# Modulation columns by transposes and a VectorE sum, and a new set of ordering numbers, in a two-layer attention backbone

## The chip, the cores and the metric

One core of a Trainium2 chip runs the whole program. The metric is the device time of one execution in microseconds (us). TensorE does matmuls and transposes, VectorE (DVE in the profile) and ScalarE (ACT) read PSUM and work on SBUF, GpSimd (POOL) works on SBUF alone, and SyncE (SP) issues most of the loads from HBM.

## The reference

Two layers work on 512 latent tokens `x` and 256 context tokens, 1024 wide. Layer 0 is differential attention with 8 heads (two softmaxes of head width 64, the second taken off with weight lambda, then a norm of each head's output). Layer 1 is grouped-query attention with 8 query heads and 2 key/value heads of width 128, norms of queries and keys, and latent outputs alone. All is in fp32.

```python
m = silu(cvec) @ ada_w[i] + ada_b[i]          # shift, scale, gate: 3 x 1024, for c and for c_ctx
h = rms_norm(x, pre_g[i]) * (1 + scale) + shift
q, k, v, z = split(h @ w_in)                  # rope on latent q and k
o = softmax(q k^T / sqrt(d)) v                # latent queries read latent and context keys
x = x + gate * rms_norm((o * silu(z)) @ w_out[i], post_g[i])
```

## The kernel before, in words

Activations are kept with features on the partitions (`h` tiles of 128 features x 768 tokens). Each large product is done as three fp32r matmuls (`mm3`, L147 to L149): both operands are split into a rounded part (`hi`) and a rest (`lo`), and hi x hi, hi x lo and lo x hi are summed in PSUM. A weight is loaded into a `raw` tile by SP, ScalarE casts it to `hi` (L210), and VectorE or GpSimd subtracts to get `lo` (L204). PSUM has eight banks: four single ones, `bk0` to `bk3`, handed out in turn (`trp` for a short use, `pj` until `close`), and two pairs `sc0`, `sc1` for scores (`sc2`). In the program's listing they are `bk_68` to `bk_71` and `sc_72`, `sc_73`.

**Start.** `x_norm` (L548) squares x on ScalarE, adds on VectorE, sums over partitions by an fp32 matmul with ones, and gets `rsb` by Ln and Exp. The modulation of layer 0 comes from `cols4`: silu(c) and silu(c_ctx) are the two columns of a 32-wide stationary tile, and four such tiles run side by side on 32 columns of the array each, so the product lies on rows 0, 1, 32, 33, 64, 65, 96, 97 of a bank. `ada_red` (L490) copies it to `row` and turns it into columns: for each block of 128 features one fp32 matmul with `row` stationary and `sel32` (128 x 2) moving adds the four partial rows and transposes at once (L497). `mods_set` adds bias and norm gain. `ht` (L574) makes an `h` tile: `hf` on VectorE (L579), `hi` on ScalarE (L580), `lo` on VectorE (L581). `w_split` (L527) splits the first weights, and `lam_setup` (L611) loads the rope table and lambda.

**Layer 0.** For each head there are score units (L845, L874: one block of 128 queries, two softmaxes; VectorE takes the maximum at L850, ScalarE the exponential at L853), then transposes of the probabilities (L910, copied to `ah` by ScalarE at L913 and to `al` by VectorE at L914), then PV matmuls (L154). L931 and L942 belong to the norm of a head's output. Projections of later heads are filled in between, and so is the modulation of layer 1 and the gate of layer 0 (`grp_mm`, L701; `ada1_finish`, L714; `gate0_finish`, L979, which broadcasts a row over the partitions with an fp32 matmul by `selb`).

**Between the layers** the output projection runs, `h1_tr` transposes the normed tokens (L1196), and a hand-written list `KV` orders key tiles `k`, value tiles `v`, transposes of the last tokens `t` and of keys `c`. A key tile holds its bank until `k_rope` has read it (`kn`, L1276), which waits for two squares on ScalarE (L1254) and two operations on GpSimd (L1256, L1257).

**Layer 1** has score units (scores L147 to L149 with `kh`, `qh`; maximum L1384, scaling of the maximum L1387, exponential L1390 into `p`), query transposes `q_tr` (L1341, cast `qh` at L1344), transposes of `p` (L1405) and PV. VectorE sums the gate of layer 1 (`gate1_part`, L1445), and `gate1_finish` splits it (cast L376 on ScalarE, subtraction L377 on GpSimd) and sums it over partitions.

**What sets the order.** A planner, `flow`, keeps its own clock in us. Each step has a due time (from `ATT`, `TS`, `AT1`, `GAP0`, `DL0`, and lags `LA`, `LT`, `LM`, `SLAG`, `SLAG1`, `QLAG`, `ACD` behind other steps); while nothing is due it takes a piece of the next projection in `FILL0` (from `HF0`) or `FILL1`. `GFIN` says after which score units `gate1_finish` may come. After that the tile framework schedules each engine's queue, led by priorities: `HOT`, `HOT0`, `HOT1`, `WARM` and `PRI` say how far a step is moved ahead. `AGB` is the number of buffers for the first modulation weights.

Of the kernel before, what the change touches and what calls it, by code (L numbers as in the profile page):

```python
# [28 lines left out]
HOT = 500
HF0 = ((('qk', 1), ('qk', 2), ('z', 0)), (('qk', 3),), (('z', 1), ('v', 2), ('qk', 4), ('z', 2)), (('qk', 5), ('z', 3)), (('v', 4), ('qk', 6), ('z', 4)), (('qk', 7), ('z', 5)), (('v', 6), ('z', 6)), (('z', 7),))  # L30
# [1 line left out]
ATT = 15.0
ACCN = (0, 0, 3, 3, 3, 3, 3, 3)
ACD = 5.0
FILL1 = (('z', 0), ('q', 2), ('q', 1), ('z', 2), ('z', 1), ('q', 3), ('z', 3), ('z', 4), ('z', 5), ('z', 7), ('z', 6))
HOT0 = (4200, 3100, 0, 4800)
HOT1 = (1100, 2900, 2600, 2600, 2100)
WARM = 5400
AGB = 11
PRE = 14.0  # L40
TS = 9.0
# [2 lines left out]
KV = (('k', 0), ('k', 1), ('k', 2), ('t', 0), ('k', 3), ('t', 1), ('v', 0), ('v', 1), ('c', 0), ('v', 2), ('c', 1), ('k', 4), ('c', 2), ('k', 5), ('c', 3), ('v', 3), ('v', 4), ('c', 4), ('v', 5), ('c', 5))
SPL = 8.0
GAP0 = 8.0
DL0 = (0.0, 0.0, 0.0, 0.0, 0.0, 0.0, -1.5, 3.0)
# [35 lines left out]
def tile_backbone(  # L83
# [406 lines left out]
    def ada_red(k0, nb, o):  # L490
        n = 2 * nb
        row = st.tile([P, 512], F32, tag="row", name=nm("row"), bufs=1)[:, :n * P]
        nc.scalar.copy(row, o)
        close(o)
        o = trp()
        for b in range(n):
            nc.tensor.matmul(o[:, b * 2:b * 2 + 2], row[:, b * P:(b + 1) * P], sel32, start=b == 0, stop=b == n - 1)  # L497
# [29 lines left out]
    def w_split(q, r):  # L527
        parts = [(wq, q * 256, 0, 256), (wk0, q * 256, 256, 256), (wv0[q // 2], q % 2 * 512, 512, 512)]
        for (hi, lo), c, a, n in parts:
            nc.scalar.copy(hi[:, c:c + n], r[:, a:a + n])  # L530
# [18 lines left out]
    rsb = st.tile([P, T], F32, name="rsb")  # L549

    def x_norm(v):
        n = (S, C)[v]
        per = 1024 // n
        a, b = ((0, S), (S, T))[v]
        o = trp()[:, :n]
        for c in range(KT // per):
# [5 lines left out]
            nc.tensor.matmul(o, ones, sq[:, :n], start=c == 0, stop=c == KT // per - 1)
# [1 line left out]
        nc.scalar.activation(rsb[:, a:b], rsb[:, a:b], AF.Exp, scale=-0.5)

# [116 lines left out]
    with tc.tile_pool(name="t0", bufs=1) as t0:  # L682
# [27 lines left out]
        def ada1_finish(layer, sec):  # L710
            r = rows.pop((layer, sec))
            o = trp()
            for b in range(4):
                nc.tensor.matmul(o[:, 2 * b:2 * b + 2], r[:, b * P:(b + 1) * P], sel32, start=b == 0, stop=b == 3)  # L714
            ov_ = o[:, :8].rearrange("p (k v) -> p v k", v=2)
# [256 lines left out]
        def gate0_finish(half):  # L972
            r = rows.pop((0, 4 + half))
            sl = slice(half * 512, half * 512 + 512)
            b = bcast(ada_b[0, 2 * D + half * 512:2 * D + half * 512 + 512])
            g = bcast(post_g[0, sl])
            for v in range(2):
                o = trp()
                nc.tensor.matmul(o, selb[v], r, start=True, stop=True)  # L979
# [674 lines left out]
```

## Time and profile before

| | us |
|---|---|
| median of 3 runs | 826.17 |
| lowest and highest | 823.46, 826.22 |
| the profiled execution | 825.35 |
| its span, first to last instruction | 823.6 |
| TensorE busy | 794.6 |
| VectorE, ScalarE, GpSimd busy | 522.8, 451.5, 319.0 |

A row of a group reads: line, engine, operation, output<-inputs, shapes, count, then busy time in us (the union of the spans), mean ns of one, and the idle time before them with what ended it. A row of the time line reads: start, duration, engine, line, operation, and in brackets the idle time before it. Matmuls overlap, so the mean of one is longer than what it adds to the busy time.

### The profile page before, as it was taken

To read this page: it belongs to the slowest core of one execution; us is meant where nothing else is said; L and a number is where in the kernel's file an instruction comes from. 1 tells how busy PE (TensorE), PEld (TensorE's weight loads), DVE (VectorE), ACT (ScalarE), POOL (GpSimd) and SP (SyncE) were. 2 spreads that over 40 slices of the span, in tenths; PEclk is the share of its full clock that TensorE was granted. 3 is DMA by queue.
4 is the path that set the end of the run, shared out by engine and by line. 5 is a ranking of instruction groups with operands and counts; after the bars stand their busy time and mean duration, and the time that the engine had idled before them with its cause. 6 is when DMAs were issued, how large, how long until landed. Compare 5 with 4: busy or idle time off the path is not lost. (4 is left out here: it accounts for less than half of the span.)

```text
span 823.6 us, 14197 instructions
## 1 busy us (share of the span) xinstructions
PE 794.6 (96%) x5436; PEld 698.8 (85%) x5436; DVE 522.8 (63%) x941; ACT 451.5 (55%) x985; POOL 319.0 (39%) x436
## 2 busy tenths in 40 slices
PE   7999999999999999999999999999999999999997
PEld 4787878798877898887988898889989899888986
DVE  3756667865869535777367952566787756665534
ACT  5524358574575643665456753564355755676631
POOL 1112544742446522363712401574446434343101
PEclk9999999999999999999999999999999999999999
DMA  9924201222143322413320042041641310111112
GB/s 344 356 75 155 88 14 53 79 76 77 35 133 128 116 78 65 142 50 133 108 94 26 27 176 81 2 135 48 198 140 51 103 52 2 61 43 52 46 32 102
DMA packets 35235, 77.75 MB, mean 94 GB/s; under 512 B 3424, under 2 KB 10336, under 8 KB 35168
## 3 DMA queue, kind: packets, MB, share of 16 engines
q1 hardware_dynamic: 31600, 71.71, 25.9%
q10 hardware_dynamic: 3568, 5.16, 1.7%
q8 instruction: 42, 0.69, 0.3%
q14 instruction: 25, 0.20, 0.1%
HBM read 70.56 MB, written 2.10 MB: 88 GB/s over the span
## 5 line engine op out<-in xcount | busy, mean ns | idle before, releaser
L147 PE MATMUL bk<-whi,h 128*128 128x256 f32 (+1 forms) x592 | 176.7, 301 | 2.0 <-DVE kn L1276 1.8
L148 PE MATMUL bk<-wlo,h 128*128 128x256 f32 (+1 forms) x592 | 175.7, 299 | 0.3 <-DVE wlo L204 0.3
L149 PE MATMUL bk<-whi,h 128*128 128x256 f32 (+1 forms) x592 | 174.1, 298 | 0.1
L147 PE MATMUL bk<-h,whi 128*128 128x512 f32 (+2 forms) x416 | 147.8, 356 | 3.9 <-ACT sq L942 1.5
L149 PE MATMUL bk<-h,wlo 128*128 128x512 f32 (+2 forms) x416 | 144.6, 348 | 0.3 <-DVE wlo L204 0.3
L148 PE MATMUL bk<-h,whi 128*128 128x512 f32 (+2 forms) x416 | 144.8, 348 | 0.0
L218 POOL TENSOR_SCALAR p<-p,sm 128x768 f32<-128x768 f32 (+1 forms) x80 | 67.9, 851 | 147.4 <-DVE sm L856 48.6
L147 PEld LDWEIGHTS bk<-whi,h 128*128 128x128 f32 x592 | 112.1, 190 | 10.8 <-issue 3.6
L148 PEld LDWEIGHTS bk<-wlo,h 128*128 128x128 f32 x592 | 112.2, 190 | 4.3 <-DVE wlo L204 0.5
L149 PEld LDWEIGHTS bk<-whi,h 128*128 128x128 f32 x592 | 111.4, 189 | 3.9 <-DVE h L1209 0.3
L204 DVE TENSOR_TENSOR wlo<-raw,whi 128x1024 fp32r<-128x1024 f32 (+2 forms) x65 | 81.3, 1250 | 42.8 <-ACT whi L210 39.2
L147 PEld LDWEIGHTS bk<-h,whi 128*128 128x128 f32 x416 | 78.1, 188 | 18.8 <-issue 4.8
L210 ACT CAST whi<-raw 128x1024 fp32r<-128x1024 f32 x64 | 67.3, 1052 | 41.6 <-PE bk L148 14.7
L149 PEld LDWEIGHTS bk<-h,wlo 128*128 128x128 f32 x416 | 78.2, 188 | 8.4 <-issue 0.8
L148 PEld LDWEIGHTS bk<-h,whi 128*128 128x128 f32 x416 | 78.3, 188 | 6.7 <-issue 0.5
L853 ACT ACTIVATE p<-sc,sm 128x768 f32<-128x768 f32 (+1 forms) x68 | 59.6, 879 | 42.3 <-DVE sm L850 42.0
L850 DVE TENSOR_REDUCE sm<-sc 128x1 f32<-128x768 f32 (+1 forms) x68 | 60.7, 917 | 17.9 <-PE sc L845 17.9
L204 POOL TENSOR_TENSOR qr<-qr,rope 128x256 f32<-128x256 f32 x28 | 27.8, 1014 | 78.7 <-DMA sw<-qr 78.0
L204 POOL TENSOR_TENSOR sz<-sz,za 128x192 f32<-128x192 f32 (+1 forms) x48 | 31.8, 683 | 62.1 <-ACT za L184 61.5
L1409 DVE TENSOR_TENSOR al<-bk,ah 128x512 fp32r<-128x512 f32 x48 | 32.1, 685 | 23.9 <-ACT ah L1408 23.0
L845 PE MATMUL sc<-qk,qk 64*128 64x384 f32 (+1 forms) x396 | 46.5, 356 | 0.2 <-POOL qk L204 0.2
L861 DVE SCALAR_TENSOR_TENSOR p<-p,sm,p 128x768 f32<-128x768 f32 (+1 forms) x34 | 39.0, 1148 | 10.7 <-POOL p L218 8.9
(236 smaller groups left out, 1678.1 us busy)
## 6 DMA issues: line engine op xcount, KB each, us to landing
raw<-in_a_w SPq DMA_DIRECT2D x28, 512.0 KB, 3.5
araw<-in_ada_w SPq DMA_DIRECT2D x12, 1024.0 KB, 5.2
raw<-in_b_w SPq DMA_DIRECT2D x20, 512.0 KB, 4.0
ag<-in_ada SPq DMA_DIRECT2D x16, 512.0 KB, 7.5
raw<-in_w_out SPq DMA_DIRECT2D x16, 512.0 KB, 3.5
sw<-qr ACTq DMA_DIRECT2D x32, 128.0 KB, 2.1
gw<-in_ada_w SPq DMA_DIRECT2D x8, 512.0 KB, 4.5
xnt<-in_xlT SPq DMA_DIRECT2D x4, 512.0 KB, 5.5
```

Of the source, the lines that this page charges most:

```text
L147: nc.tensor.matmul(o, ahi, bhi, start=start, stop=False)
L148: nc.tensor.matmul(o, ahi, blo, start=False, stop=False)
L149: nc.tensor.matmul(o, alo, bhi, start=False, stop=stop)
L204: eng.tensor_tensor(dst[:, i:i + n], a[:, i:i + n], b[:, i:i + n], op)
L210: nc.scalar.copy(hi, r)
L218: (nc.vector if eng == "v" else nc.gpsimd).tensor_scalar(dst, src, s_, 1.0, ALU.mult, ALU.mult)
L845: prev = nc.tensor.matmul(sc[m][:, j if nk == T else m, :w], a[r, tok], b[r, c], start=i == 0, stop=i == 2)
L850: nc.vector.tensor_reduce(mx, scv, AX.XY if nk == T else AX.X, ALU.max, negate=True)
L853: nc.scalar.activation(pv_, scv, AF.Exp, bias=mx, accum_out=l[:, m:m + 1])
L861: nc.vector.scalar_tensor_tensor(ps_[0], pt, r, ps_[0], ALU.mult, ALU.add)
L1409: nc.vector.tensor_tensor(al, tr, f32(ah), ALU.subtract)
```

## The change

Five edits of the code, and new values for most of the ordering numbers.

1. `row_cols` takes the place of the `sel32` matmuls in `ada_red` and `ada1_finish`: each block of 128 features is transposed whole (a 128 x 128 transpose with `ident` moving), and VectorE adds rows 0, 32, 64, 96 and rows 1, 33, 65, 97 by one reduction into a small tile, which `mods_set` and `mod_cols` then read in place of PSUM.
2. `gate0_finish` splits the row into `rh` and `rl` and does two fp32r matmuls for each one in fp32; `selb` becomes fp32r.
3. `x_norm` of the context adds its two halves on VectorE and does one matmul in place of two.
4. The casts of `w_split` are ordered after the Exp of `x_norm(0)`.
5. `lam_setup` (subg, rope table, lambda) is called one pair later in the source.

```diff
-ACD = 5.0
+ACD = 1.89
-AGB = 11
+AGB = 10
-KV = (('k', 0), ('k', 1), ('k', 2), ('t', 0), ('k', 3), ('t', 1), ('v', 0), ('v', 1), ('c', 0), ('v', 2), ('c', 1), ('k', 4), ('c', 2), ('k', 5), ('c', 3), ('v', 3), ('v', 4), ('c', 4), ('v', 5), ('c', 5))
+KV = (('k', 0), ('k', 1), ('k', 2), ('t', 0), ('v', 0), ('k', 3), ('c', 0), ('t', 1), ('v', 1), ('v', 2), ('c', 1), ('k', 4), ('c', 2), ('k', 5), ('v', 3), ('v', 4), ('c', 3), ('c', 4), ('v', 5), ('c', 5))
-SLAG = (4.5, 1.5)
-SLAG1 = 2.9
+SLAG = (4.5, -0.05)
+SLAG1 = 4.96
-GFIN = (6, 12)
+GFIN = (10, 15)
...
-        o = trp()
+        mods_set(k0, nb, row_cols(row, n).rearrange("p (w k v) -> p w v k", w=2, k=nb))
+
+    def row_cols(r, n):
+        o = trp()[:, :n * P]
         for b in range(n):
-            nc.tensor.matmul(o[:, b * 2:b * 2 + 2], row[:, b * P:(b + 1) * P], sel32, start=b == 0, stop=b == n - 1)
-        ov_ = o[:, :2 * n].rearrange("p (w k v) -> p w v k", w=2, k=nb)
-        mods_set(k0, nb, ov_)
+            nc.tensor.transpose(o[:, b * P:(b + 1) * P], r[:, b * P:(b + 1) * P], ident)
+        cols_ = small(2 * n)
+        nc.vector.tensor_reduce(
+            cols_.rearrange("p (b r) -> p b r", b=n), o.rearrange("p (b j r) -> p b r j", j=4, r=32)[:, :, 0:2, :], AX.X, ALU.add)
+        return cols_
...
-            nc.scalar.copy(hi[:, c:c + n], r[:, a:a + n])
+            with after(last[0]):
+                nc.scalar.copy(hi[:, c:c + n], r[:, a:a + n])
...
-            if v:
+            if v == 0:
+                nc.tensor.matmul(o, ones, sq[:, :n], start=c == 0, stop=c == KT // per - 1)
+            elif c:
+                nc.vector.tensor_tensor(sq[:, :512], sq[:, :512], sq0[:, :512], ALU.add)
                 nc.vector.tensor_tensor(sq[:, :n], sq[:, :n], sq[:, n:512], ALU.add)
-            nc.tensor.matmul(o, ones, sq[:, :n], start=c == 0, stop=c == KT // per - 1)
+                nc.tensor.matmul(o, ones, sq[:, :n], start=True, stop=True)
+            sq0 = sq
...
-            if pr == 1:
+            if pr == 2:
                 lam_setup()
...
+            rh, rl = (t0.tile([P, 512], F32R, tag="tmp", name=nm("rg"), bufs=3) for _ in range(2))
+            nc.scalar.copy(rh, r)
+            nc.vector.tensor_tensor(rl, r, f32(rh), ALU.subtract)
             for v in range(2):
                 o = trp()
-                nc.tensor.matmul(o, selb[v], r, start=True, stop=True)
+                nc.tensor.matmul(o, selb[v], rh, start=True, stop=False)
+                nc.tensor.matmul(o, selb[v], rl, start=False, stop=True)
```

In the built programs the instructions move as the next three places show. Line numbers of the new program are its own (up to 13 higher).

VectorE before the first `h` tile, before the change: `wlo` are the rests of the first weights, `mods` the modulation columns.

```order
L559 TENSOR_TENSOR sqx_187<-sqx_187 128x512
L204 TENSOR_TENSOR wlo_137<-raw_152,whi_136 128x256
L204 TENSOR_TENSOR wlo_139<-raw_152,whi_138 128x256
L507 SCALAR_TENSOR_TENSOR mods<-bk_71,abT 128x2
L508 TENSOR_TENSOR mods<-bk_71,abT 128x2
L509 TENSOR_TENSOR mods<-mods,pre 128x2
L579 SCALAR_TENSOR_TENSOR hf_224<-xnt,mods,rsb 128x512
L204 TENSOR_TENSOR wlo_141<-raw_152,whi_140 128x512
```

The same place after the change:

```order
L567 TENSOR_TENSOR sqx_187<-sqx_187 128x512
L502 TENSOR_REDUCE sm_211<-bk_71 128x4
L512 SCALAR_TENSOR_TENSOR mods<-sm_211,abT 128x2
L513 TENSOR_TENSOR mods<-sm_211,abT 128x2
L204 TENSOR_TENSOR wlo_137<-raw_152,whi_136 128x256
L514 TENSOR_TENSOR mods<-mods,pre 128x2
L204 TENSOR_TENSOR wlo_139<-raw_152,whi_138 128x256
L591 SCALAR_TENSOR_TENSOR hf_226<-xnt,mods,rsb 128x512
```

The reduction is new, the modulation columns come ahead of the weight rests, and the second weight rest still stands ahead of `hf`.

ScalarE at the first score units of layer 1, before the change: `ac` is the split of `gate1_finish`, `p` the exponentials, `za` a silu.

```order
L182 ACTIVATE za_6584<-za_6584 128x512
L1254 ACTIVATE jk_6619,sm_6616<-bk_68 128x128
L184 ACTIVATE za_6584<-za_6584 128x512
L376 CAST ac_7081<-gate_5212 128x512
L1390 ACTIVATE p_6648,sm_6649<-sc_73,sm_6646,qrs_6361 128x768
L1254 ACTIVATE jk_6672,sm_6671<-bk_71 128x128
```

After the change, first the same place, then the place where `ac` stands now (the sixth and the seventh exponential are around it):

```order
L182 ACTIVATE za_6613<-za_6613 128x512
L1267 ACTIVATE jk_6648,sm_6645<-bk_71 128x128
L184 ACTIVATE za_6613<-za_6613 128x512
L1403 ACTIVATE p_6683,sm_6684<-sc_73,sm_6681,qrs_6390 128x768
L1267 ACTIVATE jk_6701,sm_6700<-bk_69 128x128
...
L1435 COPY g_975_7024<-bk_68 128x256
L1403 ACTIVATE p_7013,sm_7014<-sc_72,sm_7011,qrs_6430 128x768
L376 CAST ac_7358<-gate_5241 128x512
L1403 ACTIVATE p_7070,sm_7071<-sc_73,sm_7068,qrs_6470 128x768
```

The split of the gate has moved from ahead of the first exponential to behind the sixth; GpSimd's subtraction on it moves with it.

TensorE in the list `KV`, at the last transposes of tokens, before the change. The first matmul behind them begins value tile 0 in `bk_71`, which VectorE reads for key tile 0 (`kn_5905<-bk_71`).

```order
L149 MATMUL bk_69<-whi_5815,h_672_5214 128x256
L1196 MATMUL sc_73<-ident,xn_5776 128x128 x4
L1196 MATMUL sc_72<-ident,xn_5776 128x128 x4
L147 MATMUL bk_71<-whi_5824,h_671_5213 128x256
L148 MATMUL bk_71<-wlo_5825,h_671_5213 128x256
```

After the change:

```order
L149 MATMUL bk_71<-whi_5844,h_685_5243 128x256
L1209 MATMUL sc_73<-ident,xn_5805 128x128 x4
L1209 MATMUL sc_72<-ident,xn_5805 128x128 x4
L147 MATMUL bk_69<-whi_5853,h_684_5242 128x256
L148 MATMUL bk_69<-wlo_5854,h_684_5242 128x256
```

Value tile 0 is in `bk_69`, which no key tile holds, and has begun ahead of the transposes; key tile 3 follows in `bk_70`, which VectorE reads for key tile 0 (`kn_5934<-bk_70`).

More of the change, by code (lines that the diff above doesn't have):

```diff
@@ L28 @@
 SC_B = 128 ** -0.5
[L29 to L30 removed]
+HOT = 682
+HF0 = ((('qk', 1), ('z', 0), ('qk', 2)), (('qk', 3),), (('z', 1), ('v', 2), ('qk', 4), ('z', 2)), (('qk', 5),), (('z', 3), ('v', 4), ('qk', 6), ('z', 4)), (('qk', 7),), (('v', 6), ('z', 5), ('z', 6)), (('z', 7),))
 FILL0 = tuple(f for hf in HF0 for f in hf)
[L32 to L41 removed]
+ATT = 15.35
+ACCN = (0, 0, 3, 2, 4, 3, 3, 3)
+ACD = 1.89
+FILL1 = (('z', 0), ('q', 1), ('z', 2), ('q', 2), ('z', 1), ('q', 3), ('z', 4), ('z', 3), ('z', 5), ('z', 7), ('z', 6))
+HOT0 = (4682, 4208, 950, 4318)
+HOT1 = (1476, 3151, 2600, 3076, 2271)
+WARM = 4385
+AGB = 10
+PRE = 16.26
+TS = 9.04
 HFD = 2
 KVE = (0, 1, 0, 1)
[L44 to L47 removed]
+KV = (('k', 0), ('k', 1), ('k', 2), ('t', 0), ('v', 0), ('k', 3), ('c', 0), ('t', 1), ('v', 1), ('v', 2), ('c', 1), ('k', 4), ('c', 2), ('k', 5), ('v', 3), ('v', 4), ('c', 3), ('c', 4), ('v', 5), ('c', 5))
+SPL = 4.41
+GAP0 = 6.86
+DL0 = (0.0, 0.0, 0.0, 0.0, 0.0, 0.98, -1.5, 2.26)
 WBUFS = 3
@@ L52 @@
 WX = (1, 1)
-LA = (7.0, 7.0)
-LT = (1.2, 1.6)
+LA = (9.48, 6.98)
+LT = (1.27, 1.44)
 AHEAD = 2
-SLAG = (4.5, 1.5)
-SLAG1 = 2.9
-AT1 = 9.0
+SLAG = (4.5, -0.05)
+SLAG1 = 4.96
+AT1 = 9.83
 EGL = 'v'
@@ L63 @@
 EWL = 'vppp'
-PRI = (1500, 300, 400, 0)
-GFIN = (6, 12)
-QLAG = 4.0
-QTR = 2.0
+PRI = (1500, 300, 495, 398)
+GFIN = (10, 15)
+QLAG = 4.66
+QTR = 1.92
 EG0 = 'v'
@@ L73 @@
 EGA = "v"
-LM = (4.5, 4.5)
+LM = (4.56, 5.53)
 AB = 3
@@ L457, in tile_backbone @@
     nc.vector.tensor_reduce(sel32, ident.rearrange("p (j r) -> p r j", j=4)[:, 0:2, :], AX.X, ALU.add)
-    selb = [cp.tile([P, P], F32, name=f"selb{v}", bufs=1) for v in range(2)]
+    selb = [cp.tile([P, P], F32R, name=f"selb{v}", bufs=1) for v in range(2)]
     for v in range(2):
@@ L549, in tile_backbone @@
     rsb = st.tile([P, T], F32, name="rsb")
+    last = {}
     def x_norm(v):
@@ L556, in x_norm @@
         for c in range(KT // per):
-            sq = st.tile([P, 1024], F32, tag="sqx", name=nm("sqx"), bufs=2)
+            sq = st.tile([P, 1024], F32, tag="sqx", name=nm("sqx"), bufs=3)
             nc.scalar.activation(sq.rearrange("p (k n) -> p k n", k=per), xnt[:, c * per:c * per + per, a:b], AF.Square)
             nc.vector.tensor_tensor(sq[:, :512], sq[:, :512], sq[:, 512:], ALU.add)
-            if v:
+            if v == 0:
+                nc.tensor.matmul(o, ones, sq[:, :n], start=c == 0, stop=c == KT // per - 1)
+            elif c:
+                nc.vector.tensor_tensor(sq[:, :512], sq[:, :512], sq0[:, :512], ALU.add)
                 nc.vector.tensor_tensor(sq[:, :n], sq[:, :n], sq[:, n:512], ALU.add)
-            nc.tensor.matmul(o, ones, sq[:, :n], start=c == 0, stop=c == KT // per - 1)
+                nc.tensor.matmul(o, ones, sq[:, :n], start=True, stop=True)
+            sq0 = sq
         nc.scalar.activation(rsb[:, a:b], o, AF.Ln, scale=1.0 / D, bias=eps)
-        nc.scalar.activation(rsb[:, a:b], rsb[:, a:b], AF.Exp, scale=-0.5)
+        last[v] = nc.scalar.activation(rsb[:, a:b], rsb[:, a:b], AF.Exp, scale=-0.5)
     def pri(f, i):
@@ L711, in ada1_finish @@
             r = rows.pop((layer, sec))
[L712 to L715, printed above, removed]
+            ov_ = row_cols(r, 4).rearrange("p (k v) -> p v k", v=2)
             mod_cols(layer, sec % 2, sec // 2, lambda v: ov_[:, v, :])
```

## Prediction

> **What bounds the kernel now.** I read the page first: how full TensorE is, and at which clock.
>
> ```profile
> PE 794.6 (96%) x5436; PEld 698.8 (85%) x5436; DVE 522.8 (63%) x941; ACT 451.5 (55%) x985; POOL 319.0 (39%) x436
> PEclk9999999999999999999999999999999999999999
> ```
>
> TensorE is busy for 794.6 of 823.6 us, at full clock. What is left to win is its own work and 29.0 us in which it has nothing to do. Next the stretches, to see where the 29 us lie (columns: stretch, its length, busy us of each engine, clock, DMA share, GB/s).
>
> ```profile
> 0.00:25.00 25.00, 20.68 (x109) 12.67 (x110) 9.29 (x29) 13.19 (x23) 3.74 (x10) 0.93 0.96 348
> 425.00:450.00 25.00, 23.01 (x169) 20.93 (x168) 20.14 (x39) 16.76 (x39) 6.99 (x9) 1.00 0.07 22
> 450.00:475.00 25.00, 22.68 (x169) 21.10 (x170) 21.59 (x37) 19.61 (x42) 8.68 (x11) 1.00 0.07 22
> 550.00:575.00 25.00, 23.06 (x190) 22.30 (x189) 16.14 (x42) 11.94 (x38) 14.90 (x21) 1.00 0.14 43
> 600.00:625.00 25.00, 22.57 (x169) 21.59 (x167) 22.13 (x44) 13.17 (x38) 15.45 (x20) 1.00 0.39 128
> 800.00:825.00 25.00, 17.65 (x124) 16.39 (x122) 9.87 (x18) 3.96 (x14) 4.25 (x15) 0.95 0.23 84
> ```
>
> The start idles 4.3 us (25 - 20.68) and the last stretch, which ends at 823.6, 5.95; the tail is not edited. Four stretches in between lose 1.9 to 2.4 us each. The waits of TensorE by releaser say what they are (waiting line, then the releaser; us in total, times, longest).
>
> ```profile
> PE sc L147 <- ACT p L1390: 4.1, 5, 1.6
> PE bk L910 <- DVE al L914: 3.3, 4, 1.8
> PE bk L147 <- DVE kn L1276: 1.8, 2, 0.9
> PE sc L147 <- ACT h L580: 1.5, 1, 1.5
> PE bk L147 <- ACT sq L942: 1.5, 1, 1.5
> PE sc L147 <- ACT qh L1344: 1.0, 1, 1.0
> ```
>
> These are all waits for a PSUM bank or an operand that another engine reads or makes; no weight load is among these six. So the time is set by TensorE's work plus how well the order covers the other engines' chains.
>
> **The work that changes.** The built programs differ on TensorE in three things only: 32 matmuls with sel32 become 32 transposes, four fp32 matmuls with selb become eight fp32r ones, and one fp32 matmul of x_norm(1) goes. Groups by line and shape (busy us, mean ns; an fp32 matmul leaves two records, a transpose one):
>
> ```profile
> L497 PE MATMUL bk<-sel,row 128*128 128x2 f32 x32 | 4.0, 241 | 0.8 <-ACT row L493 0.8
> L714 PE MATMUL bk<-sel,arow 128*128 128x2 f32 x32 | 3.8, 240 | 0.0
> L1405 PE MATMUL bk<-ident,p 128*128 128x128 f32 x192 | 28.4, 273 | 0.0
> L1341 PE MATMUL bk<-ident,q 128*128 128x128 f32 x32 | 5.4, 272 | 0.0
> L979 PE MATMUL bk<-arow,selb 128*128 128x512 f32 x8 | 4.2, 605 | 0.0
> L378 PE MATMUL bk<-ac,ones_r 128*128 128x512 f32 x2 | 0.8, 397 | 0.0
> L562 PE MATMUL bk<-sqx,ones 128*128 128x256 f32 x4 | 1.3, 418 | 0.3 <-DVE mods L508 0.3
> ```
>
> The sel32 matmuls take 4.0 + 3.8 = 7.8 us. A transpose costs 28.4/192 = 0.148 (L1405) to 5.4/32 = 0.169 (L1341), so 32 cost 4.7 to 5.4: -2.4 to -3.1, I take -2.8. The selb matmuls go from 4.2 to 8 x 0.8/2 = 3.2: -1.0. x_norm(1): half of 1.3, -0.65. Together -4.4. Busy spans overlap their neighbours, so part may not be time; with half of the first term the sum is -3.0, and that is my lower bound. The upper bound is -4.8.
>
> What is added elsewhere: nine small VectorE sums, two 512-wide subtractions and one 512-wide add; two ScalarE casts of 512. None stands on TensorE's path except at the start, below. DMA: subg, rope and lambda now stand on SP ahead of all of the last modulation pair's loads, not among them; about 0.66 MB, at the start's 348 GB/s 1.9 us by which a load of pair 3 lands later. One ag buffer fewer adds a wait of SP, with the later ada and weight loads queued behind it. TensorE has other pairs' matmuls at that time, so I price both at nothing; without that cover 1.9 us.
>
> **The start.** The first h tile:
>
> ```profile
> 13.62 0.41 ACT L530 CAST whi<-raw 128x256 fp32r<-128x256 f32 x1
> 13.93 0.64 ACT L564 ACTIVATE rsb<-rsb 128x512 f32<-128x512 f32 x1
> 14.06 0.42 DVE L204 TENSOR_TENSOR wlo<-raw,whi 128x256 fp32r<-128x256 f32 x1 [0.15 <-ACT whi L530]
> 14.89 0.75 DVE L579 SCALAR_TENSOR_TENSOR hf<-xnt,mods,rsb 128x512 f32<-128x512 f32 x1
> 16.45 0.78 PE L147 MATMUL sc<-h,whi 128*128 128x512 f32 x2 [1.50 <-ACT h L580]
> ```
>
> The weight casts now wait for the Exp of x_norm(0), and two of them that stood before it, one per 0.31 us (13.93 - 13.62), go behind it: Exp starts at 13.3 and ends at 13.95. In the new VectorE order both wlo subtractions, which need these casts, still stand before hf: the second cast ends near 14.67, its subtraction of 0.42 near 15.1, and hf starts there instead of at 14.89: +0.2. x_norm(1) now has sum, add and add in one chain before its only matmul: some +0.5 more wait. From none (all covered) to +1.5 (both half as long again, plus a late load); I take +0.5.
>
> **The scores of layer 1.** The first wait, 1.63 us:
>
> ```profile
> 608.45 0.94 DVE L1384 TENSOR_REDUCE sm<-sc 128x1 f32<-128x768 f32 x1
> 609.94 1.66 POOL L377 TENSOR_TENSOR ac<-gate,ac 128x512 fp32r<-128x512 f32 x1
> 610.38 1.23 DVE L1387 TENSOR_TENSOR sm<-sm,qrs 128x1 f32<-128x1 f32 x1
> 611.70 0.99 ACT L1390 ACTIVATE p<-sc,sm,qrs 128x768 f32<-128x768 f32 x1 [1.84 <-DVE sm L1387]
> 612.84 0.45 PE L147 MATMUL sc<-kh,qh 128*128 128x384 f32 x1 [1.63 <-ACT p L1390]
> L1387 DVE TENSOR_TENSOR sm<-sm,qrs x32: 133/152/1231, 610.4 to 758.3; 128x1 f32<-128x1 f32 x32
> ```
>
> L1387 takes 0.15 in the median and 1.23 here: it ends at 611.61, as GpSimd's L377 of gate1_finish does (609.94 + 1.66 = 611.60). The new order puts that cast and subtraction behind the sixth exponential: -1.1 at this wait. The Trainium skill, SBUF — State Buffer, "Who interferes with whom", says that a VectorE instruction with two SBUF inputs and a GpSimd one that reads SBUF lock each other out for a whole instruction. By that rule, which the two ends bear out, the stall can move along with L377 to the new place; this wait would then bring 0 instead of -1.1, and the time be 818.
>
> The other waits here come from score units that follow the last but one too soon. Counted in the two orders, at 0.12 us for a matmul of 256 columns and in proportion for others, the nearest pair lies 2.8 us apart before and 3.8 now, and the wait for qh (1.0) gets more than 3 us of matmuls as cover. For these I take -1.4, so -2.5 in all, half of 4.1 + 1.0 (bounds 0 and -5.1).
>
> **The keys of layer 1.** One of the two waits for kn:
>
> ```profile
> 551.54 0.28 PE L147 MATMUL bk<-whi,h 128*128 128x256 f32 x1
> 551.66 0.28 PE L148 MATMUL bk<-wlo,h 128*128 128x256 f32 x1
> 553.24 0.61 DVE L1276 SCALAR_TENSOR_TENSOR kn<-bk,qrs,gq 128x128 f32<-128x128 f32 x2 [3.29 <-POOL qrs L1257]
> 553.90 0.39 PE L147 MATMUL bk<-whi,h 128*128 128x256 f32 x1 [0.88 <-DVE kn L1276]
> ```
>
> After the transposes the first v tile needs the bank of key tile 0. In the new order that v tile has a free bank and has begun; 13 of its matmuls, 13 x 0.12 = 1.6 us, come before the next tile asks for the old bank. That covers 0.88. For the second wait the new order leaves as little room as the old one: it stays. -0.9 (bounds +0.5 and -1.8).
>
> **Layer 0.** The longest single wait:
>
> ```profile
> 428.52 1.82 DVE L850 TENSOR_REDUCE sm<-sc 128x1 f32<-128x768 f32 x2
> 430.32 0.68 DVE L914 TENSOR_TENSOR al<-bk,ah 128x512 fp32r<-128x512 f32 x1
> 431.06 0.66 PE L910 MATMUL bk<-ident,p 128*128 128x128 f32 x4 [1.82 <-DVE al L914]
> ```
>
> The transposes want a bank whose copy (al) stands behind two maxima. This is between heads 6 and 7, where no projection is ready to fill in. The new table leaves such a stretch too (scores, modulation matmuls and PV alone), so I leave 1.8 there. The other three waits for al and the one for sq (1.5) came where a bank was asked for again within 0.8 us of its last use. In heads 0 and 1 the new order has no such place left; the sq bank gets 0.7 us of other work as cover, where it had none. But heads 6 and 7 gain two places where matmuls follow the transposes that feed them within 1 us. Of 3.3 + 1.5 and the small ones beside them I take -2.0 net; bounds -5 and +3.6 (two more waits like the 1.8).
>
> **Sum**, against the profiled execution's 825.35 us (span 823.6 and 1.75 around it): -4.4 + 0.5 - 2.5 - 0.9 - 2.0 = -9.3, so 816.05. The runs' median is 826.17, 0.8 above the profiled one: 816.9, said as 817. What is late next is the dense stretch between heads 6 and 7.
>
> **Rivals.**
>
> *Only the work is saved.* Waits of one order go and others of the same size come. For it: the idle time lies in small pieces over the whole span, and a table of numbers moves all of them. Against it: the wider score spacing and the free bank stand in the order. 825.35 - 4.4 + 0.8 = 821.8.
>
> *Slower: the bank wait of head 6 becomes the rule.* SLAG for the context units falls from 1.5 to -0.05 and ACD from 5.0 to 1.89, so score units and modulation steps come closer behind PV steps; each time transposes then wait for al behind two maxima, 1.82 is lost. Eight heads give 14.6: 821.8 + 14.6 = 836. To be slower by over 4.1 us (0.5%, about what a measurement of this kernel tells from no change) it takes (830.3 - 821.8)/1.82 = 4.7, so five heads. Against it: in the new order most score units are followed by projection matmuls, as before.
>
> *Transposes let the clock drop.* The start has 0.93 granted; 7% of 25 us is 1.75 us. Were that lost again at each of the seven groups of four that the change adds, 12 us would come on top: 821.8 + 12 = 834. Against it: L910's transposes run in 425 to 475 at 1.00. The Trainium skill, TensorE: Matmul & The Clock Gate, "PE-mode transpose", says that transposes do not count as busy for the clock gate, which speaks against this change; no stretch here shows a drop.
>
> **How the numbers follow.** Forecast 0.62; only the work 0.24; head 6's wait 0.11; the clock 0.01; 0.02 for things that I do not name, near no change. The line for faster is 826.17 - 4.1 = 822.0. Of the forecast 0.59 lie below it (its own range is 810 to 823), of the second case, which sits on the line, 0.11. Faster 0.70, same 0.03 + 0.13 + 0.02 = 0.18, slower 0.12. The range leaves out most of the slower cases and the best tenth: 809 to 826.
>
> **What would show it.** Right: L714 and L497 gone, 32 transposes near 5 us busy; no L1387-like instruction of 1.2 us before the second score unit of layer 1; waits for p under 2.5 us; one wait for kn left. Wrong: waits of transposes for al above 5 us in total, an idle start above 5.5 us, or TensorE's busy time down by less than 3.

## The result, and the profile after

The changed kernel takes 800.49 us (median of 4 runs, lowest 799.04), the kernel before 825.38 beside it: ratio 0.9696 [0.9669, 0.9723]. The forecast was 817 with a range of 809 to 826: the sign holds, the size does not. One of the four executions, the profiled one, took 1520.42 us with TensorE at about half rate (without it the median is 800.38, and the ratio leaves it out), so the profile shown is that of a second measurement of the same kernel (e1), 801.60 us with a span of 799.8.

The page of the changed kernel:

```profile
PE 777.7 (97%) x5402; PEld 691.7 (86%) x5402; DVE 530.3 (66%) x952; ACT 451.7 (56%) x987; POOL 325.7 (41%) x436
PEclk9999999999999999999999999999999999999999
```

TensorE's busy time fell by 794.6 - 777.7 = 16.9 us, its idle time only from 29.0 to 799.8 - 777.7 = 22.1. The forecast had looked for 4.4 in work and 4.9 in waits. The stretches (columns as before):

```profile
0.00:25.00 25.00, 18.18 (x105) 10.29 (x106) 9.36 (x30) 13.20 (x23) 3.77 (x10) 1.00 0.96 349
25.00:50.00 25.00, 22.31 (x145) 16.62 (x144) 18.00 (x37) 10.28 (x22) 7.07 (x8) 0.93 0.71 267
425.00:450.00 25.00, 23.57 (x161) 20.91 (x160) 20.41 (x37) 20.46 (x44) 10.50 (x15) 1.00 0.13 43
450.00:475.00 25.00, 25.00 (x211) 24.91 (x210) 17.94 (x29) 17.09 (x40) 5.96 (x6) 1.00 0.34 122
550.00:575.00 25.00, 24.30 (x201) 24.10 (x202) 17.08 (x35) 9.76 (x32) 9.57 (x14) 1.00 0.48 158
600.00:625.00 25.00, 24.45 (x179) 23.57 (x178) 19.02 (x44) 16.27 (x38) 15.03 (x22) 1.00 0.20 63
```

The stretches that lost 1.9 to 2.4 us each now lose 0 to 1.4 (they are stretches of time, and other work stands in them now). The two at the start idle more than before. TensorE's waits:

```profile
PE bk L573 <- DVE mods L513: 2.1, 1, 2.1
PE sc L147 <- ACT h L592: 2.0, 2, 1.6
PE bk L466 <- DMA ag<-in_ada: 1.8, 2, 1.3
PE bk L569 <- DVE sqx L567: 1.8, 3, 1.0
...
PE bk L154 <- DVE al L923: 0.8, 1, 0.8
...
PE sc L147 <- ACT p L1403: 0.6, 1, 0.6
```

The first four rows are all the start. Of the six waits that the prediction named, five are gone or below 1 us: p from 4.1 to 0.6, al ahead of transposes from 3.3 to none, kn, sq and qh gone; only h stays.

### The profile page after: what moved, and what is told of

It is laid out like the page before. It is cut to its first block, busy times and chain, and to the rows that moved or that the text cites. A ratio compares the mean times of both kernels' runs of the same rounds, so it can differ in the third digit from the quotient of the medians.

```text
span 1518.6 us, 14146 instructions
## 1 busy us (share of the span) xinstructions
PE 1508.1 (99%) x5402; PEld 1227.0 (81%) x5402; DVE 528.8 (35%) x952; ACT 460.8 (30%) x987; POOL 305.2 (20%) x436
## 4 chain that ended last, share of the span: by engine, by line
PE 98%; DMA 1%; issue 0%; DVE 0%; ACT 0%; POOLq 0%; DVEq 0%; SPq 0%; POOL 0%
PE bk L147 20%; PE bk L149 20%; PE bk L148 20%; PE bk L154 10%; PE sc L854 5%; PE bk L919 3%; PE sc L147 3%; PE sc L149 3%; PE sc L148 3%; PE bk L1418 3%; PE bk L713 2%; PE bk L466 1%; PE sc L883 1%; PE sc L1209 1%; PE bk L1354 0%; PE bk L500 0%
## 5 line engine op out<-in xcount | busy, mean ns | idle before, releaser
L147 PE MATMUL bk<-whi,h 128*128 128x256 f32 (+1 forms) x592 | 279.9, 476 | 0.0
L148 PE MATMUL bk<-wlo,h 128*128 128x256 f32 (+1 forms) x592 | 279.0, 472 | 0.0
L149 PE MATMUL bk<-whi,h 128*128 128x256 f32 (+1 forms) x592 | 277.4, 473 | 0.0
L147 PE MATMUL bk<-h,whi 128*128 128x512 f32 (+2 forms) x416 | 243.6, 586 | 0.0
L149 PE MATMUL bk<-h,wlo 128*128 128x512 f32 (+2 forms) x416 | 241.0, 580 | 0.0
L148 PE MATMUL bk<-h,whi 128*128 128x512 f32 (+2 forms) x416 | 238.8, 574 | 0.0
L147 PEld LDWEIGHTS bk<-whi,h 128*128 128x128 f32 x592 | 197.1, 334 | 25.7 <-issue 21.4
L149 PEld LDWEIGHTS bk<-whi,h 128*128 128x128 f32 x592 | 196.6, 334 | 16.7 <-issue 13.7
L148 PEld LDWEIGHTS bk<-wlo,h 128*128 128x128 f32 x592 | 197.7, 334 | 14.2 <-issue 12.5
L149 PEld LDWEIGHTS bk<-h,wlo 128*128 128x128 f32 x416 | 130.6, 314 | 32.8 <-issue 28.6
L148 PEld LDWEIGHTS bk<-h,whi 128*128 128x128 f32 x416 | 130.5, 314 | 31.6 <-issue 27.0
L147 PEld LDWEIGHTS bk<-h,whi 128*128 128x128 f32 x416 | 126.0, 303 | 36.7 <-issue 31.9
L204 DVE TENSOR_TENSOR wlo<-raw,whi 128x1024 fp32r<-128x1024 f32 (+2 forms) x65 | 78.7, 1210 | 128.3 <-ACT whi L210 128.3
L854 PE MATMUL sc<-qk,qk 64*128 64x384 f32 (+1 forms) x396 | 74.3, 536 | 0.0
L854 PEld LDWEIGHTS sc<-qk,qk 64*128 64x128 f32 x396 | 47.2, 265 | 26.7 <-issue 20.2
L919 PE MATMUL bk<-ident,p 128*128 128x128 f32 x224 | 64.0, 444 | 0.0
```

The source lines that it names most:

```text
L147: nc.tensor.matmul(o, ahi, bhi, start=start, stop=False)
L148: nc.tensor.matmul(o, ahi, blo, start=False, stop=False)
L149: nc.tensor.matmul(o, alo, bhi, start=False, stop=stop)
L204: eng.tensor_tensor(dst[:, i:i + n], a[:, i:i + n], b[:, i:i + n], op)
L854: prev = nc.tensor.matmul(sc[m][:, j if nk == T else m, :w], a[r, tok], b[r, c], start=i == 0, stop=i == 2)
L919: nc.tensor.transpose(tr[:, e * 256 + i * P:e * 256 + (i + 1) * P], a[:, j * P:(j + 1) * P], ident)
```

## The experiments

Two theories at first. **Order**: the new numbers take away waits, many of which the busy time hides. **Work**: the edits of the code save more than their busy rows show. All ratios are to the kernel before, run beside each. The runs come from four chips (e1 to e4, e5 to e8, e9 to e12, e13 to e18) on which the kernel before has medians of 824.85 to 826.62, so differences of about 1 us across these groups say nothing.

| run | what it is | median us | ratio [95%] |
|---|---|---|---|
| e1 | the changed kernel again | 800.21 | 0.9684 [0.9656, 0.9713] |
| e2 | code edits, all old numbers | 835.46 | 1.0114 [1.0091, 1.0138] |
| e3 | new numbers, old code | 806.34 | 0.9763 [0.974, 0.9785] |
| e4 | new, but layer 0's numbers old | 826.70 | 1.0004 [0.9987, 1.0021] |
| e5 | new, but fills of layer 0 old | 816.31 | 0.9889 [0.9875, 0.9904] |
| e6 | new, but lags of layer 0 old | 820.47 | 0.9935 [0.9917, 0.9954] |
| e7 | new, but priorities of layer 0 old | 811.21 | 0.9831 [0.9816, 0.9845] |
| e8 | new, but norm of the context old | 798.40 | 0.9675 [0.966, 0.969] |
| e9 | new, but layer 1's numbers old | 808.58 | 0.9808 [0.9792, 0.9825] |
| e10 | new, but sel32 matmuls back | 807.48 | 0.9786 [0.9772, 0.9801] |
| e11 | before, SLAG and ACD new | 825.89 | 1.0009 [0.9995, 1.0022] |
| e12 | new, but all of the start old | 799.89 | 0.9695 [0.9681, 0.971] |
| e13 | as e8, beside e14 | 798.68 | 0.9665 [0.9641, 0.969] |
| e14 | the changed kernel, beside e13 | 800.66 | 0.9682 [0.9655, 0.9709] |
| e15 | new, but selb in fp32 | 800.82 | 0.9692 [0.9663, 0.972] |
| e16 | new, but SLAG and ACD old | 805.16 | 0.974 [0.9714, 0.9767] |
| e17 | as e2, but sel32 matmuls back | 826.68 | 1.0019 [1.0004, 1.0034] |
| e18 | as e2, but norm of the context old | 833.69 | 1.0106 [1.0084, 1.0128] |

**Code or numbers (e1 to e4, e9).** e1 is the changed kernel without an edit.

> The changed kernel once more, for a profile in the state of its other runs. Both theories: 799 to 801 us. Order theory (the new numbers remove waits that the busy time of TensorE hides, because its spans overlap): TensorE's busy time falls by about 5 us, but its idle time by under 15, and the rest is in the spacing of its matmuls. Work theory (the edits of the code save more TensorE time than the busy time of the replaced matmuls): the spacing of the other matmuls is as before.

800.21, as both theories had it. TensorE's busy time fell by 16.9 us, where the order theory had expected about 5.

e2 is the changed kernel with every ordering number as before:

```diff
-HOT = 682
+HOT = 500
...
-LM = (4.56, 5.53)
+LM = (4.5, 4.5)
```

> The five edits of the code with all ordering numbers of before. Order theory: 818 to 823 us, a ratio to before of 0.991 to 0.997, since only 3 to 5 us of work go. Work theory: under 812 us, ratio under 0.984.

Both theories missed: 835.46, slower by 1.1%. The code alone costs 9 us. Its trace shows one place at the end of layer 0. First what the other engines do, then TensorE:

```profile
457.69 4.47 POOL L204 TENSOR_TENSOR gT<-gT,sz 128x256 f32<-128x256 f32 x3 [3.42 <-DVE gT L954]
462.19 0.86 ACT L824 COPY sz<-bk 128x384 f32<-128x384 f32 x2 [1.97 <-POOL gT L204]
465.92 0.91 ACT L862 ACTIVATE p<-sc,sm 128x768 f32<-128x768 f32 x1
```

```profile
462.72 0.33 PE L919 MATMUL bk<-ident,p 128*128 128x128 f32 x1 [1.23 <-ACT sz L824]
466.97 1.01 PE L854 MATMUL sc<-qk,qk 64*128 64x256 f32 x6 [3.92 <-ACT p L862]
469.41 0.58 PE L147 MATMUL sc<-whi,h 128*128 128x256 f32 x1 [1.02 <-ACT p L862]
469.79 0.41 PE L148 MATMUL sc<-wlo,h 128*128 128x256 f32 x1
```

ScalarE waits 1.97 for GpSimd, with the exponentials queued behind that copy; TensorE stands for 1.23 + 3.92 + 1.02 = 6.2 us. And the matmuls behind take 0.41 instead of 0.28. The granted clock in the same kernel:

```profile
460.00:465.00 5.00, 1.82 (x14) 1.43 (x12) 5.00 (x5) 3.03 (x8) 2.16 (x2) 0.92 0.31 105
465.00:470.00 5.00, 2.00 (x10) 1.49 (x10) 4.64 (x8) 4.76 (x10) 0.91 (x1) 0.50 0.00 0
470.00:475.00 5.00, 5.00 (x27) 5.00 (x26) 3.65 (x10) 2.02 (x6) 3.59 (x5) 0.55 0.01 3
475.00:480.00 5.00, 5.00 (x46) 4.73 (x45) 3.36 (x9) 2.48 (x7) 0.48 (x1) 1.00 0.00 0
```

From 470 to 475 there are 27 matmuls where the next 5 us hold 46: the wait is paid a second time through the clock.

e3 is the reverse, old code with the new numbers:

```diff
-HOT = 500
+HOT = 682
...
-LM = (4.5, 4.5)
+LM = (4.56, 5.53)
```

> The new ordering numbers with the code of before. Order theory: 802 to 810 us, ratio 0.972 to 0.981. Work theory: 815 to 823 us, ratio 0.987 to 0.997. If the two parts need each other, both this and the code alone stay above 815.

806.34, inside the order theory's 802 to 810. This kernel has exactly the instructions of before on TensorE. Its page:

```profile
PE 783.1 (97%) x5436; PEld 696.4 (87%) x5436; DVE 526.8 (66%) x941; ACT 449.2 (56%) x985; POOL 323.5 (40%) x436
```

The same 5436 matmuls are busy 783.1 instead of 794.6 us. Those 11.5 us are no work. About 2 of them come from the clock: in the first 25 us, where 0.93 was granted before and 1.00 here, 20.68 us were busy before and 18.78 here. For the rest, look at how matmuls are drawn. A 256-column matmul is drawn 0.28 long and followed 0.12 later by the next, so a wait of up to 0.16 leaves no gap, and a longer one shows 0.16 too little. By their starts: take for each matmul the distance to the next start, take off the usual one (0.11 for up to 128 columns, 0.12 for 256, 0.175 for 384, 0.23 for 512) and 0.04 more, and add up what is left over: 64.1 us before, 48.6 here, 15.5 less, while the visible idle time falls by 8.2, from 29.0 to 803.9 - 783.1 = 20.8. The other 7.3 us were waits that the drawing hides. The Trainium skill, Perfetto Trace Analysis, "Identifying the Most-Contended Engine", says that matmul busy share is no good measure of headroom and names two others, one of them the busy share of weight loads; the trace agrees, since PEld's 698.8 against 696.4 us hardly moves.

e4 is the changed kernel with layer 0's numbers as before (HOT, HF0, ATT, ACCN, ACD, HOT0, WARM, SPL, GAP0, DL0, SLAG, and the first of LA, LT, LM), and e9 with layer 1's:

```diff
-LA = (9.48, 6.98)
+LA = (7.0, 6.98)
-SLAG = (4.5, -0.05)
+SLAG = (4.5, 1.5)
...
```

> The edits of the code, the new numbers of layer 1, the list of keys and the priorities of the start; the numbers of layer 0 as before. Order theory: the gain of the numbers lies in both layers, so 808 to 814 us. If layer 0 holds nearly all of it: over 816. If layer 1 holds nearly all of it: under 804. Work theory: no further from the changed kernel than 5 us.

```diff
-LA = (9.48, 6.98)
+LA = (9.48, 7.0)
-SLAG1 = 4.96
+SLAG1 = 2.9
-GFIN = (10, 15)
+GFIN = (6, 12)
...
```

> The changed kernel with layer 1's numbers as before (KV, FILL1, HOT1, TS, SLAG1, AT1, GFIN, QLAG, QTR, the second of LA, LT, LM); layer 0's new. The prediction priced these numbers at 2.5 for the scores and 0.9 for the keys: 803 to 804. Theory that each wait of the old order is lost whole (p 4.1, qh 1.0, kn 1.8, and the short waits that TensorE's busy time hides): 8 to 10, so 808 to 811, with waits for p above 3 and for kn above 1.5 in the trace. Rival, layer 1 is worth nothing once layer 0 is mended: within 1 of 800.

Layer 0's numbers bring 826.70 - 800.21 = 26.5 with the new code (e4, whose trace has the same 6.2-us chain as e2), layer 1's 808.58 - 800.5 = 8.1 (800.5: the middle of the changed kernel's medians). 826.70 fits the theory by which layer 0 holds nearly all of the gain, but e9 shows that layer 1 has a part of its own. In e9 the waits of before are back, nearly one for one:

```profile
PE sc L147 <- ACT p L1403: 3.3, 6, 1.2
...
PE bk L147 <- DVE kn L1289: 1.8, 2, 0.9
...
PE sc L147 <- ACT qh L1357: 1.0, 1, 1.0
```

So in layer 1 each named wait was time. From the first transposes of tokens (L1209) to the end, e9 takes 805.4 - 504.5 = 300.9 us and e1 799.8 - 506.9 = 292.9. Of these 8.0 us the three rows hold 6.1 - 0.6 = 5.5 (0.6 is what is left of the wait for p in e1); where the other 2.5 stand is not shown.

**Which numbers of layer 0 (e5, e6, e7, e11, e16).** Three thirds put back one at a time:

```diff
-HF0 = ((('qk', 1), ('z', 0), ('qk', 2)), (('qk', 3),), (('z', 1), ('v', 2), ('qk', 4), ('z', 2)), (('qk', 5),), (('z', 3), ('v', 4), ('qk', 6), ('z', 4)), (('qk', 7),), (('v', 6), ('z', 5), ('z', 6)), (('z', 7),))
+HF0 = ((('qk', 1), ('qk', 2), ('z', 0)), (('qk', 3),), (('z', 1), ('v', 2), ('qk', 4), ('z', 2)), (('qk', 5), ('z', 3)), (('v', 4), ('qk', 6), ('z', 4)), (('qk', 7), ('z', 5)), (('v', 6), ('z', 6)), (('z', 7),))
-ACCN = (0, 0, 3, 2, 4, 3, 3, 3)
+ACCN = (0, 0, 3, 3, 3, 3, 3, 3)
```

> The changed kernel with HF0 and ACCN (order of layer 0's fills, modulation steps per head) as before; layer 0's lags and priorities stay new. Three theories on the 26 us that layer 0's numbers bring with the new code. Fills: which projection stands behind which score unit decides; then 812 to 826, and the waits of transposes for al (0.8 us now) are above 2.5. Lags: 799 to 806. Priorities: 799 to 806. None alone (the numbers fit one another, and any third put back costs most of it): above 812 here and in the two next runs.

```diff
-ATT = 15.35
+ATT = 15.0
-ACD = 1.89
+ACD = 5.0
...
-LA = (9.48, 6.98)
+LA = (7.0, 6.98)
```

> The changed kernel with layer 0's due times and lags (ATT, ACD, SPL, GAP0, DL0, SLAG, and the first of LA, LT, LM) as before; fills and priorities new. Lags: 812 to 826, waits for al above 2.5. Fills or priorities: 799 to 806. The prediction's slower rival held that SLAG and ACD as changed cost time; by it this kernel is faster than the changed one, below 799.

```diff
-HOT = 682
+HOT = 500
-HOT0 = (4682, 4208, 950, 4318)
+HOT0 = (4200, 3100, 0, 4800)
-WARM = 4385
+WARM = 5400
```

> The changed kernel with HOT, HOT0 and WARM as before (how far the framework moves layer 0's steps ahead on each engine); fills and lags new. TensorE's own order hardly depends on them, so fills and lags say 799 to 806. Priorities: 812 to 826, with waits for the maxima and exponentials, which other work on VectorE and ScalarE then stands ahead of.

816.31, 820.47, 811.21: each third costs 11 to 20 us, together 16 + 20 + 11 = 47 where all at once cost 26.5. The fourth theory holds best, no third alone (811.21 is just below its line of 812): the numbers fit one another. The waits in e6 say how a misfit looks, one long one and some of 0.8 to 1.6:

```profile
PE bk L147 <- DVE al L923: 3.3, 1, 3.3
PE bk L919 <- DVE al L923: 3.0, 3, 1.6
...
PE bk L154 <- ACT ah L922: 1.8, 2, 1.5
```

The two numbers of the prediction's slower rival, alone in the old kernel (e11) and put back alone in the new (e16):

```diff
-ACD = 5.0
+ACD = 1.89
-SLAG = (4.5, 1.5)
+SLAG = (4.5, -0.05)
```

> The kernel before with only SLAG = (4.5, -0.05) and ACD = 1.89, the two numbers of the prediction's slower rival (context score units and modulation steps closer behind PV steps). The rival: transposes wait for al behind two maxima in five or more heads, 830 or above, waits for al of 8 or more. Theory that the numbers only work as one set: 822 to 830. Theory that the lags alone take waits away: 812 to 820.

```diff
-ACD = 1.89
+ACD = 5.0
-SLAG = (4.5, -0.05)
+SLAG = (4.5, 1.5)
```

> The changed kernel with SLAG and ACD alone as before. The prediction's slower rival: faster than the changed kernel. Nothing as in the old set: within 1 of 800. Part of the set: 803 to 810, with waits for al or ah in layer 0 that the changed kernel lacks.

825.89 in the old set: nothing. 805.16 in the new set, against 800.66 beside it: they are worth 4.5 there. The rival has fallen on both counts.

**The edits of the code (e10, e17, e15).** `row_cols` with the old matmuls, in the new set (e10) and in the old (e17):

```diff
...
-            nc.tensor.transpose(o[:, b * P:(b + 1) * P], r[:, b * P:(b + 1) * P], ident)
-        cols_ = small(2 * n)
...
-        return cols_
+            nc.tensor.matmul(o[:, b * 2:b * 2 + 2], r[:, b * P:(b + 1) * P], sel32, start=b == 0, stop=b == n - 1)
+        return o[:, :2 * n]
```

> The changed kernel with the 32 matmuls by sel32 (fp32, two records each) back in place of the 32 transposes and their sums. The prediction's term: 2.8 slower, so 803.0 (802.3 to 803.4). Spacing theory: from start to start 64 records of the old kernel took 3.5 + 3.4 = 6.9 us and 32 transposes 0.109 each, 3.5: 3.4 slower, 803.6. Rival, the sums on VectorE that the transposes need stand on the path at the start and take it back: 800 or less.

> All old numbers and the code edits, but with the sel32 matmuls in place of the transposes and their VectorE sums. Theory that the transposes' sums shift VectorE's order at the end of layer 0: the 6.2-us chain of waits there goes and the time is 826 to 829 (the norm's loss at the start stays). Rival, any edit shifts it: 832 or more.

In the new set the transposes are worth 807.48 - 800.5 = 7.0, in the old set they cost 835.46 - 826.68 = 8.8. All three expectations of e10 missed. What the transposes save in instructions is the same in both sets. The rows of the changed kernel, first and last start among the columns:

```profile
L500 PE MATMUL bk<-ident,row x16: 272/272/299, 13.5 to 55.7; 128*128 128x128 f32 x16
L500 PE MATMUL bk<-ident,arow x16: 270/272/329, 310.8 to 420.1; 128*128 128x128 f32 x16
```

Two groups of 2.6 us busy (by the groups by shape) stand where 4.0 + 3.8 were: 2.6 saved. The rest is order. In the old set e17 shows where: its trace has the old waits again, 1.8 for al, 1.5 for sq, 4.0 for p, and the 6.2-us chain of e2 is gone. This edit put the old numbers out of fit; the other four together cost 826.68 - 825.29 = 1.4 there. By which step of the framework's scheduling is not shown, and neither is which waits make the rest of the 7.0 in the new set: of the 6.0 us between the traces of e10 and e1, 1.7 lie ahead of the first scores of layer 0 and 4.1 between them and the first transposes of tokens.

selb in fp32 again (e15), without the cast and subtraction:

```diff
...
-                nc.tensor.matmul(o, selb[v], rh, start=True, stop=False)
-                nc.tensor.matmul(o, selb[v], rl, start=False, stop=True)
+                nc.tensor.matmul(o, selb[v], r, start=True, stop=True)
```

> The changed kernel with the four fp32 selb matmuls of gate0_finish back in place of eight fp32r ones, and without the cast and the subtraction that make rh and rl. The prediction's term: 1.0 slower. Spacing theory: 8 records took 2.8 us from start to start and the 8 new ones 1.9, so 0.9 slower, 801. Rival, the two 512-wide operations that go with it stand on paths of ScalarE and VectorE and cost as much: 799 to 800. If it is 5 or more, any edit of the code puts the numbers out of fit, and the 7 us of the sel32 run are of that kind.

800.82 against 800.66: not told apart from nothing. This edit left the fit alone, so not every edit upsets it.

**The norm of the context (e8, e12, e13, e14, e18).**

```diff
-            if v == 0:
-                nc.tensor.matmul(o, ones, sq[:, :n], start=c == 0, stop=c == KT // per - 1)
-            elif c:
-                nc.vector.tensor_tensor(sq[:, :512], sq[:, :512], sq0[:, :512], ALU.add)
+            if v:
                 nc.vector.tensor_tensor(sq[:, :n], sq[:, :n], sq[:, n:512], ALU.add)
-                nc.tensor.matmul(o, ones, sq[:, :n], start=True, stop=True)
-            sq0 = sq
+            nc.tensor.matmul(o, ones, sq[:, :n], start=c == 0, stop=c == KT // per - 1)
```

> The changed kernel with the norm of the context as before (two fp32 matmuls, no 512-wide add between). Start theory: the add of 0.69 us and the second sum lie on the chain to the first h tile of the context, the wait ahead of the norm's matmul (2.1 us) falls to 0.6 as in the kernel with new numbers and old code, the clock between 30 and 40 us goes from 0.83 back to 1.00, and the time is 2.2 us less: 797 to 799. Rival: the loads of the modulation weights end last at the start, the wait moves to them, and the time stays at 800 (within 0.7).

798.40. The time line of the changed kernel shows the edit's chain, and what follows it:

```profile
27.60 0.69 DVE L567 TENSOR_TENSOR sqx<-sqx 128x512 f32<-128x512 f32 x1 [1.87 <-ACT sqx L566]
28.33 0.69 DVE L571 TENSOR_TENSOR sqx<-sqx,sqx 128x512 f32<-128x512 f32 x1
29.05 0.42 DVE L572 TENSOR_TENSOR sqx<-sqx 128x256 f32<-128x256 f32 x1
29.62 0.67 PE L573 MATMUL bk<-sqx,ones 128*128 128x256 f32 x2 [2.12 <-DVE mods L513]
...
32.45 0.42 PE L148 MATMUL bk<-wlo,h 128*128 128x256 f32 x1
...
33.22 1.92 PE L466 MATMUL bk<-ag,s 128*32 128x512 f32 x8
```

With the old norm (e3 here, which has the new numbers and the other old code too) the matmul comes 0.65 earlier, and the same matmuls behind it are faster; in e8, where the norm alone is old, it starts at 28.74, 0.88 earlier:

```profile
28.97 0.67 PE L562 MATMUL bk<-sqx,ones 128*128 128x256 f32 x2 [0.59 <-DVE mods L508]
...
31.43 0.28 PE L148 MATMUL bk<-wlo,h 128*128 128x256 f32 x1
...
32.58 1.07 PE L466 MATMUL bk<-ag,s 128*32 128x512 f32 x8
```

The wait of 2.12 costs 0.65 itself and again through the clock: 0.42 instead of 0.28 for a matmul, 1.92 instead of 1.07 for a group of eight. e13 and e14 ran the two side by side:

> The changed kernel with the old norm of the context, beside the changed kernel itself (next run) on one chip. Start theory: 2.2 us faster than that one (1.5 to 3.5), the intervals apart. Rival, the earlier 1.8 us between calls were the chip's: within 1 us.

> The changed kernel once more, to compare with the run ahead of it and the two behind it: 799.5 to 801.5.

798.68 and 800.66, 2.0 apart as the theory says, though the two intervals of the ratios overlap. One of e14's four runs, 798.18, is below all of e13's. Two pairs of medians (798.4 and 800.2, 798.7 and 800.7) and the time lines agree, so I take the 2 us as real: the first scores of layer 0 start at 82.1 in e1 and at 80.0 in e8. The lower clock is the larger part of it. In e9 and e5, which have the new norm, the wait ahead of its matmul was 0.7, the clock stayed at 1.00 behind it, and the first scores start at 80.7. The kernel with the old norm is then the fastest of this study. With the rest of the start put back as well (old casts, old rope loads, 11 buffers):

```diff
-AGB = 10
+AGB = 11
...
-            with after(last[0]):
-                nc.scalar.copy(hi[:, c:c + n], r[:, a:a + n])
+            nc.scalar.copy(hi[:, c:c + n], r[:, a:a + n])
...
-            if pr == 2:
+            if pr == 1:
                 lam_setup()
```

> The changed kernel with the whole start as before but for the transposes: old norm of the context, casts of the first weights free, rope and lambda loads at pair 1, 11 buffers for the modulation weights. If the wait of TensorE for ag (1.3 us at 20.9 us) is time, 1.0 to 1.5 below the kernel with the old norm alone: 796 to 798. If the four edits but the norm are free, as the prediction had it: 798 to 799. If the late rope loads were worth something, above 799.

799.89: not below e8, although the longest wait for ag fell from 1.3 to 0.7 us, so that wait was no time, and the three edits are worth 0 to 1.5. That the late rope loads gain something, as the expectation had it for a time above 799, is not shown by a difference this small. Last, the old norm in the old set:

> All old numbers and the code edits, but with the old norm of the context. The start's loss goes (2 to 4 us) and the chain at the end of layer 0 stays: 831 to 834. If the chain goes as well, 823 to 826: then the end of layer 0 hangs on where the start put the framework's queues, and no edit has a price of its own.

833.69 against 835.46, and the 6.2-us chain stays. The new norm costs about 2 us in either set.

## Why the prediction was right in sign and wrong in size

**The step that failed first** is the sentence "What is left to win is its own work and 29.0 us in which it has nothing to do". It took busy time for work. e3 took 11.5 us out of the busy time with the same instructions, so the part to be won was larger than the rows of waits showed, and even the sum of all lower bounds (-4.8 + 0 - 5.1 - 1.8 - 5 = -16.7) would have missed -25.

**The work, -4.4.** As instructions it was right: 7.8 to 5.2 for the columns, and the selb matmuls 4.2 to 3.3 (two groups of 1.7 and 1.6). As time it was not: the columns are worth 7.0 in this set and cost 8.8 in the old one, selb is not measurable, and the norm loses 2 us instead of saving 0.65. The step priced an edit by its instructions where its effect was on the order of the other engines.

**The start, +0.5.** The first `h` tile was right. Its matmul starts at 16.57 instead of 16.45:

```profile
16.57 0.73 PE L147 MATMUL sc<-h,whi 128*128 128x512 f32 x2 [1.55 <-ACT h L592]
```

The norm of the context was mis-sized: some 0.5 of wait against 0.65 of work saved, so about nothing; it costs about 2, some 0.7 by the wait and the rest by the clock (80.0, 80.7 and 82.1 above). That a wait in a sparse stretch can be paid twice, through the clock, was not in the sum. The prediction's sign of failure "idle start above 5.5 us" came (25 - 18.18 = 6.8) and meant little: the same stretch was at clock 1.00 where it had been 0.93, so about as many matmuls (105 against 109) were busy for less, and part of the time was waited out again for a load (ag, 1.34 us at 22.27).

**Layer 1, -2.5 and -0.9.** The mechanism was right and the size off: 8.1 by e9 where -3.4 was forecast. Of the waits for p and qh, 5.1 us, half was taken; 4.5 went. The stall of L1387 at this wait did go when `gate1_finish` moved, and in e9, where it is back in its old place, a stall of 1.24 us is back with it. The rival that let the whole 1.2 us move along did not come true, since no such instruction falls on L377 in the new place. The longest is now 0.60:

```profile
L1400 DVE TENSOR_TENSOR sm<-sm,qrs x32: 136/151/598, 593.8 to 735.0; 128x1 f32<-128x1 f32 x32
```

That one ends at 727.17, and a GpSimd instruction (L204) that began before it ends at 727.15. So the trace agrees with the Trainium skill, SBUF — State Buffer, "Who interferes with whom", by which a VectorE instruction with two SBUF inputs and a GpSimd one that reads SBUF lock each other out. One wait for kn was to stay; none did.

**Layer 0, -2.0.** This is the largest miss, and a term of the sum that was mis-sized. "Heads 6 and 7 gain two places", each like the 1.82, did not happen, nor did the 1.82 stay that was left there: no wait of transposes for al of 0.3 us or more is left. The starts of two instructions divide each trace into three parts (first scores of layer 0, L845 or in the new code L854; first transposes of tokens, L1196 or L1209). One execution each, in us:

| | to the first scores | from there to the first transposes | from there to the end |
|---|---|---|---|
| before | 80.0 | 441.4 | 302.2 |
| the changed kernel (e1) | 82.1 | 424.8 | 292.9 |
| new numbers, old code (e3) | 80.1 | 429.9 | 293.9 |
| old numbers, new code (e2) | 83.1 | 449.1 | 301.4 |
| as e2, but sel32 matmuls back (e17) | 81.0 | 441.3 | 302.1 |
| new, but layer 0's numbers old (e4) | 81.9 | 450.2 | 293.2 |
| new, but layer 1's numbers old (e9) | 80.7 | 423.8 | 300.9 |

The middle part, nearly all layer 0, is 16.6 us shorter, of which the work of the columns of layer 1 and of selb explains 2.1; the last part is 9.3 shorter and the first 2.1 longer. The two layers hardly touch each other: e9 has the middle part of the changed kernel, and e4 its last part. What layer 0's numbers bring depends on the code they meet: 11.5 with the old code (e3), 25.4 with the new (e4 against e1), since in this part the new code costs 7.7 with the old numbers (e2 against before; with the sel32 matmuls back, e17, nothing) and saves 5.1 with the new ones (e3 against e1). Which of the short waits behind the 11.5 is how much stays open.

**The rivals.** "Only the work is saved" fell: numbers without a code edit bring 20 us. "Head 6's wait becomes the rule" fell by e11 and e16. The clock rival was right that a lower clock could follow the change, for the wrong reason: e10 has matmuls in place of transposes at this spot and the same 0.93 from 25 to 50 us, e8 has the transposes and 1.00. The idle time of TensorE does it, as the last section works out: 1.89 us of the 3.41 us ahead of e10's drop, 0.96 at that place in e8. By the rule of the Trainium skill, TensorE: Matmul & The Clock Gate, "PE-mode transpose", that transposes do not count as busy, e8 should be nearer to a drop than e10; no run here tests that with the idle time alike.

## What to carry to other kernels

Judge the room that an order leaves by the distance from start to start of like matmuls, not by busy share and visible gaps: here 64 us stood between the matmuls, while 29 were visible as idle time, and the new numbers alone took 15.5 of the 64 away. Ordering numbers tuned as a set belong to one code: price an edit together with a renewed set, since the same edit gained 7 us with one and lost 9 with the other. And when several edits come in one change, take the cheap ones back one by one afterwards; here the norm of the context was a loss inside a large gain.
